# Adding U1 into two banks at mid-block, and giving out mLSTM's key scaling and turn at other steps, in a hybrid mLSTM and DeltaNet layer

## The chip, the cores and the metric

One NeuronCore of a Trainium2 chip runs the whole layer in one launch. Its engines work side by side, each on its own stream of instructions: TensorE (PE in the profile; PEld is its weight load), VectorE (DVE), ScalarE (ACT), GpSimd (POOL) and SyncE (SP, here only a queue that issues DMAs). They wait for each other by semaphores. The metric is the device time of one execution in microseconds (us), as the median of several runs.

## The reference: one layer on 512 tokens of width 2048

A layer normalises x, projects it once, runs two token mixers on the parts of that projection, projects both results back, gates and merges them, adds the residual and normalises. All is fp32, for one batch of 512 tokens and D_MODEL 2048.

```python
IN_SIZES = (ML_QK_WIDTH, ML_QK_WIDTH, ML_WIDTH, ML_WIDTH, ML_WIDTH, ML_HEADS, ML_HEADS,
            3 * DN_WIDTH, DN_WIDTH, DN_HEADS, DN_HEADS,
            D_MODEL, D_MODEL)
...
def _mlstm_chunkwise(q, k, v, i_pre, logf):
...
        num = (inter_w[..., None] * jnp.einsum('bhtd,bhde->bhte', q_c, C)
               + jnp.einsum('bhts,bhse->bhte', intra_w, v_c))
...
        kw = k_c * jnp.exp(we_c - m_new[..., None])[..., None]
        C_new = decay[..., None, None] * C + jnp.einsum('bhsd,bhse->bhde', kw, v_c)
```

The mLSTM has 8 heads with keys of 128 and values of 256; the DeltaNet 16 heads of 128. Most of the work is the two projections: 2048 by some 20,500 columns in, 4096 by 2048 out.

## The kernel before: seven products instead of eight, and a clock of steps

**Precision.** Every fp32 operand of a projection is split into a high and a low part in a format that TensorE multiplies fast; a product of two is then three matmuls (high by high, high by low, low by high). ScalarE casts the high part of a weight tile (L135, `wh`), VectorE subtracts to get the low part (L138, `wl`), from raw tiles that SP loads (`wr`). `uh` and `ul` are the two parts of the normalised input.

**Seven-product blocks.** Nine blocks of two times 512 columns (4 of kind "z", 2 "v", 3 "g": the list SEVEN) are projected by a form of Strassen-Winograd multiplication: the 512 tokens are two halves, the 2048 rows of the weights eight pairs of tiles, and a block of 2 x 2 quarter products is computed with seven products. Each block walks eight quads of group A, with products m6, m1, m5 and m7 each, and then eight quads of group B, with m1, m5 and m7 only, added into the same banks. Each product has two token tiles t of three matmuls of 128x512, so 56 products in all. The operands of group A need sums of the inputs (`suh`, `sul`, `s4h`, `s4l`, made by `u_sums` before the blocks) and sums of weight tiles (`t13`, `ts`, L526, L527), one of which goes to DRAM (`t_d`) and is read again by group B (L533).

All eight PSUM banks of a core are in use by one block: m6 has two (`pso`), and m1, m5 and m7 have two each (`psj` and `psw`). Results are sums of the products. U1[t] and C22[t] are two pairs of tiles in SBUF. At the end of group A, m6 is copied to U1 (L562, ScalarE); then VectorE makes U1 += m1, C22 = U1 + m5 and C22 += m7 (all by `add`, L558). The banks of m1, m5 and m7 go on collecting through group B. At the block's end VectorE adds U1 into m5's banks (m5 = U1 + m5) and m7's to U1 (U1 += m7), and the sinks write out four results per t: m1's bank, m5's bank, C22 and U1, with an activation on ScalarE. The last products of a block come in another order (the last two quads' m1 and m5 before their m7), so that banks of the next block come free early.

**Order.** TensorE's order is the order in which the code calls it, written by hand. The other engines' order comes from a scheduler with priorities: `urgent(n)` raises that of what is inside, loads and splits of the blocks have a high one, and `behind("V")` holds an instruction until the newest split on that engine has been issued. Work beside the products is written as generators: `start(gen, wait)` enters one in a list, and `tick()`, called after each product and each group of projection matmuls, lets each go on to its next `yield n`, n ticks later. So numbers of ticks decide where such work is put against TensorE's.

**mLSTM.** A unit treats two heads j. `ml_start` turns the keys of both heads (by `turn`: a transpose of blocks on VectorE, L774, then four stores to DRAM, L784, and four ticks later one load back, L789) and loads v. `ml_prep` makes decay weights (`em`, L1063) and scores (`psc`, L1068). `ml_rec` scales the turned keys (`kw`, L1087) and runs over four chunks c: `pnum` (L1092) from the scores and the state, and `pcs` (L1098), which needs the scaled keys, for the state of the next chunk. `ml_fin` turns the result out. The first unit (`ml_first`, heads 0 and 1) begins right behind the last seven-product block from keys and queries computed earlier; the other three follow between the DeltaNet units, whose projections (`proj_cm`, L249 to L251, copied from their banks to `yp` at L740) fill TensorE in the meantime.

Of the kernel before, what the change touches and what calls it, by code (L numbers as in the profile page):

```python
# [56 lines left out]
def hybrid_body(  # L57
# [82 lines left out]
    def behind(eng):  # L140

        return tc.issue_after(newest[eng])
# [67 lines left out]
    def start(gen, wait=0):  # L210
        active.append([gen, clock["t"] + wait])
# [167 lines left out]
    def u_sums():  # L379
        for i in range(KH):  # L380
            uf, sf = X[:, 0, :, :], X[:, 1, :, :].rearrange("p a (b n) -> p (a b) n", n=HP)
            V.tensor_tensor(out=uf, in0=uh[:, 2 * i:2 * i + 2, :].bitcast(F32), in1=ul[:, 2 * i:2 * i + 2, :].bitcast(F32),
                            op=ALU.add)
            a11, a21, a12, a22 = uf[:, 0, 0:HP], uf[:, 0, HP:S], uf[:, 1, 0:HP], uf[:, 1, HP:S]
            G.tensor_tensor(out=sf[:, 0], in0=a21, in1=a22, op=ALU.add)
            G.tensor_tensor(out=sf[:, 1], in0=sf[:, 0], in1=a11, op=ALU.subtract)
            G.tensor_tensor(out=sf[:, 2], in0=a11, in1=a21, op=ALU.subtract)
            G.tensor_tensor(out=sf[:, 3], in0=a12, in1=sf[:, 1], op=ALU.subtract)
            yield 3
            for hi, lo, src in ((suh[:, i], sul[:, i], sf[:, 0:3]), (s4h[:, i], s4l[:, i], sf[:, 3])):  # L390
                A.copy(hi, src)
                V.tensor_tensor(out=lo, in0=src, in1=hi.bitcast(F32), op=ALU.subtract)
            yield 2

    acol = cp.tile([P, NC, MLH], F32, tag="acol", name="acol")
    emcol = cp.tile([P, NC, MLH], F32, tag="emcol", name="emcol")
# [159 lines left out]
    def add(x, a, b):  # L556
        with urgent(3):
            V.tensor_tensor(out=x, in0=a, in1=b, op=ALU.add)  # L558

    def copy1(t, p1):  # L560
        with urgent(3):
            A.copy(U1[t], p1)  # L562

    def seven(n0, kind, c1, c2):

        m6, m1, m5, m7 = ([pool.tile([P, NO], F32, tag=t, name="ps") for pool, t in banks_] for banks_ in (OO, JW, JW, JW))
        ends = {"A": (lambda t: copy1(t, m6[t]), lambda t: add(U1[t], U1[t], m1[t]),
                      lambda t: add(C22[t], U1[t], m5[t]), lambda t: add(C22[t], C22[t], m7[t])),
                "B": SINK[kind](c1, c2, m1, m5, m7, n0 + 2 * KH == len(quads))}

        def product(n, m):
            g, i = "AB"[n // KH], n % KH
            ps = ((m6, m1, m5, m7) if g == "A" else (m1, m5, m7))[m]
            hi, lo = partq[n0 + n][m]
            for t in range(2):
                ah, al = LHS[g][m](i, slice(t * P, (t + 1) * P))
                T.matmul(ps[t], ah, hi, start=(g == "A" and i == 0), stop=False, skip_group_check=True)  # L577
                T.matmul(ps[t], ah, lo, start=False, stop=False, skip_group_check=True)  # L578
                T.matmul(ps[t], al, hi, start=False, stop=(i == KH - 1), skip_group_check=True)  # L579
                if i == KH - 1 and ends[g][m] is not None:  # L580
                    ends[g][m](t)
            tick()

        N = 2 * KH
        for n in range(N - 2):
            prep_sums(n0 + n + 1)
            prep_pair(n0 + n + 1)
            load_quad()
            if n == N - 3:

                prep_sums(n0 + n + 3)
            for m in range(4 if n < KH else 3):
                if n == N - 3 and m == 2:
                    prep_sums(n0 + N - 1)
                    prep_pair(n0 + N - 1)
                product(n, m)

        load_quad()
        last = n0 + N == len(quads)
        for n, m in ((N - 2, 0), (N - 2, 1), (N - 1, 0), (N - 1, 1), (N - 2, 2), (N - 1, 2)):  # L600
            if (n, m) == (N - 1, 0):
                prep_pair(n0 + N)
                load_quad()
            if last and (n, m) == (N - 1, 1):
                limit[0] = len(plan)
                prepare(nfront - 1)
            product(n, m)
# [4 lines left out]
    def sink_flat(dst, func, scale):  # L612

        def sink(c1, c2, m1, m5, m7, last):
            def out_(ps, c, col):
                o = spare(last)
                with urgent(3):
                    A.activation(o, ps, func, scale=scale)
                nc.scalar.dma_start(dst(c, col), o)

            def late(x_, c, col):
                with behind("A"):
                    if func != AF.Copy:
                        A.activation(x_, x_, func, scale=scale)
                    nc.scalar.dma_start(dst(c, col), x_)
                yield 1

            def end5(t):
                add(m5[t], U1[t], m5[t])
                out_(m5[t], t, c2)  # L630
                start(late(C22[t], 2 + t, c2), 1)

            def end7(t):
                add(U1[t], U1[t], m7[t])
                start(late(U1[t], 2 + t, c1), 2)

            return (lambda t: out_(m1[t], t, c1)), end5, end7
        return sink

    def sink_z(c1, c2, m1, m5, m7, last):  # L640

        col = c1 - ML_Z
        zs, os_ = {}, {}

        def end1(t):
            zs[t] = spare(False)
            with urgent(3):
                A.copy(zs[t], m1[t])

        def end5(t):  # L650
            add(m5[t], U1[t], m5[t])
            os_[t] = spare(False)
            with urgent(3):
                A.activation(os_[t], m5[t], AF.Tanh, scale=0.5)
            start(late(zs[t], os_[t], t), 5 + 5 * t)

        def late(z, o, c):
            th = spare(True)
            with behind("A"):
                A.activation(th, z, AF.Tanh, scale=0.5)  # L660
                if c > 1:
                    A.activation(o, o, AF.Tanh, scale=0.5)
            with behind("V"):
                V.scalar_tensor_tensor(out=z, in0=th, scalar=1.0, in1=z, op0=ALU.add, op1=ALU.mult)
            yield 2
            with behind("V"):
                V.scalar_tensor_tensor(out=z, in0=o, scalar=1.0, in1=z, op0=ALU.add, op1=ALU.mult)
            yield 2
            with behind("A"):
                nc.scalar.dma_start(g_d[c, :, col:col + NO], z)  # L670

        def end7(t):
            add(U1[t], U1[t], m7[t])
            start(late(U1[t], C22[t], 2 + t), 14 + 5 * t)

        return end1, end5, end7

    SINK = {"g": sink_flat(lambda c, col: tg_d[c, :, col - GATE:col - GATE + NO], AF.Tanh, 0.5),
            "v": sink_flat(lambda c, col: v_d[c, :, col - ML_V:col - ML_V + NO], AF.Copy, 1.0),
# [53 lines left out]
    def bc(col, n):  # L733
        return col.unsqueeze(2).to_broadcast([P, NC, n])
# [316 lines left out]
    def ml_prep(j, hs, kq, u):  # L1051
# [25 lines left out]
        G.tensor_tensor(out=qi, in0=qi, in1=iwb, op=ALU.mult)  # L1077
        u["em"].append((w, we, de, qi))

    def ml_rec(j, hs, kq, u):  # L1080
        h = hs[j]
        v1 = u["v1"][j]
        kT = kq[j][:, 0, :]
        w, we, de, qi = u["em"][j]
        kw = u["kw"][j]
        with behind("V"):
            V.tensor_tensor(out=kw, in0=kw, in1=bc(we, P), op=ALU.mult)  # L1087
        sq = wk.tile([P, NC], F32, tag="sq", name="sq")
        c1 = None
        for c in range(NC):  # L1090
# [18 lines left out]
            jk = wk.tile([P, NB], F32, tag="jk", name="mjk", bufs=1)  # L1109
            A.activation(jk, v1[:, c, 0:NB], AF.Square, accum_out=sq[:, c:c + 1])  # L1110
            if c == NC - 2:
                g = [wk.tile([P, NC, P], F32, tag="g", name="mg", bufs=4) for _ in range(2)]
                for i in range(2):
                    col = h * NB + i * P
                    nc.sync.dma_start(g[i], g_d[:, :, col:col + P].rearrange("c p n -> p c n"))
# [25 lines left out]
    def ml_both(hs, kq, u):  # L1141
        for j in range(2):
            yield from ml_prep(j, hs, kq, u)
        for j in range(2):
            yield from ml_rec(j, hs, kq, u)
            yield from ml_fin(j, hs, u)

    def ml_start(hs, kq, u):
        for j in range(2):
            kw = wk.tile([P, NC, P], F32, tag="ke", name="kw", bufs=4)  # L1150
            turn(kq[j][:, 0, :], kw)
            u["kw"].append(kw)
            v1 = wk.tile([P, NC, NB + 1], F32, tag="aq", name="v1", bufs=4)
            G.memset(v1[:, :, NB:NB + 1], 1.0)
            nc.sync.dma_start(v1[:, :, 0:NB], v_d[:, :, hs[j] * NB:(hs[j] + 1) * NB].rearrange("c p n -> p c n"))
            u["v1"].append(v1)
# [6 lines left out]
    def ml_first(hs, kq, u):  # L1163

        for j in range(2):
            for i in range(2):
                nc.sync.dma_start(kq[j][:, 1 - i, :], qk_d[2 * i + j])
        yield 4
        with behind("V"):
            ml_start(hs, kq, u)  # L1170
        yield 5
        yield from ml_both(hs, kq, u)

    def ml_unit(p):
# [186 lines left out]
```

## Time and profile before

| | us |
|---|---|
| median of 3 runs | 2278.94 (2275.77 to 2279.93) |
| the profiled execution | 2278.73 |
| its span, first to last instruction | 2276.9 |
| TensorE busy in the span | 2218.0 |
| the nine seven-product blocks | 136 to 843 from the span's start |
| first mLSTM unit | from 850 |

In the rows of a group, "x72 | 46.0, 679" means 72 instructions, 46.0 us in all, 679 ns each. Names left and right of the arrow are what is written and read, then come partitions x elements. X stands for a tile of a name with a number (U1, C22). On a timeline, the first two numbers are the start in us from the span's start and the duration, and what stands in brackets is the idle time of the engine ahead of the instruction, and what ended it. A row of the windows view has the length of a stretch, then the busy time of PE, PEld, DVE, ACT and POOL with counts, the clock granted to TensorE as a share of the full one, the DMA engines' share and GB/s. Matmuls are pipelined: their durations overlap, and what one costs is the distance between starts.

### The profile page before, as it was taken

To read this page: it belongs to the slowest core of one execution; us is meant where nothing else is said; L and a number is where in the kernel's file an instruction comes from. 1 tells how busy PE (TensorE), PEld (TensorE's weight loads), DVE (VectorE), ACT (ScalarE), POOL (GpSimd) and SP (SyncE) were. 2 spreads that over 40 slices of the span, in tenths; PEclk is the share of its full clock that TensorE was granted. 3 is DMA by queue.
4 is the path that set the end of the run, shared out by engine and by line. 5 is a ranking of instruction groups with operands and counts; after the bars stand their busy time and mean duration, and the time that the engine had idled before them with its cause. 6 is when DMAs were issued, how large, how long until landed. Compare 5 with 4: busy or idle time off the path is not lost.

```text
span 2276.9 us, 32977 instructions
## 1 busy us (share of the span) xinstructions
PE 2218.0 (97%) x11600; PEld 1858.0 (82%) x11600; DVE 1507.5 (66%) x2725; ACT 893.3 (39%) x1776; POOL 248.3 (11%) x325
## 2 busy tenths in 40 slices
PE   7999999999999999999999999999999999999998
PEld 5888888778778778788888888888888899978886
DVE  5967798777777757776496846867376855334445
ACT  4434444444444443343343434434334334232223
POOL 0500000000000001211021202212022100000111
PEclk9999999999999999999999999999999999999999
DMA  5366666667767757557565746658366556764333
GB/s 157 88 190 188 212 195 213 195 197 232 225 186 221 244 180 201 132 120 197 121 165 121 185 124 155 149 121 204 100 159 144 129 144 201 243 206 149 115 116 131
DMA packets 503464, 384.50 MB, mean 169 GB/s; under 512 B 238337, under 2 KB 402402, under 8 KB 503298
## 3 DMA queue, kind: packets, MB, share of 16 engines
q1 hardware_dynamic: 406018, 333.03, 52.5%
q10 hardware_dynamic: 97280, 49.37, 7.4%
q8 instruction: 91, 1.49, 0.3%
q14 instruction: 75, 0.61, 0.1%
HBM read 309.86 MB, written 72.42 MB: 168 GB/s over the span
## 4 chain that ended last, share of the span: by engine, by line
PE 75%; DMA 9%; DVE 8%; issue 3%; SPq 2%; ACT 1%; POOL 0%; ACTq 0%; DVEq 0%; POOLq 0%
PE pj L249 12%; PE pj L250 11%; PE pj L251 11%; PE ps L578 7%; PE ps L577 6%; PE ps L579 6%; PE py L1295 3%; PE py L1296 3%; PE py L1294 3%; DVE wl L138 3%; DMA wr<-in_w_in_dram 2%; DMA wr<-t_d 2%; PE pjt L264 2%; PE pjt L266 2%; PE pjt L267 2%
## 5 line engine op out<-in xcount | busy, mean ns | idle before, releaser
L138 DVE TENSOR_TENSOR wl<-wr,wh 128x512 fp32r<-128x512 f32 (+1 forms) x624 | 487.2, 786 | 346.0 <-ACT wh L135 336.0
L135 ACT CAST wh<-wr 128x512 fp32r<-128x512 f32 (+1 forms) x624 | 415.6, 669 | 760.3 <-PE pj L250 351.8
L249 PE MATMUL pj<-uh,wh 128*128 128x512 f32 x1280 | 531.1, 415 | 3.2 <-ACT yp L740 3.2
L251 PE MATMUL pj<-uh,wl 128*128 128x512 f32 x1280 | 501.8, 392 | 0.0
L250 PE MATMUL pj<-ul,wh 128*128 128x512 f32 x1280 | 501.3, 392 | 0.0
L251 PEld LDWEIGHTS pj<-uh,wl 128*128 128x128 f32 x1280 | 241.1, 188 | 53.0
L249 PEld LDWEIGHTS pj<-uh,wh 128*128 128x128 f32 x1280 | 242.0, 189 | 49.0 <-ACT yp L740 4.0
L250 PEld LDWEIGHTS pj<-ul,wh 128*128 128x128 f32 x1280 | 242.1, 189 | 43.1
L578 PE MATMUL ps<-wl,uh 128*128 128x512 f32 x432 | 170.6, 395 | 7.1 <-DVE wl L138 7.1
L577 PE MATMUL ps<-wh,uh 128*128 128x512 f32 x432 | 169.6, 393 | 2.5 <-DVE X L558 2.3
L579 PE MATMUL ps<-wh,ul 128*128 128x512 f32 x432 | 168.3, 390 | 0.0
L578 PE MATMUL ps<-wl,suh 128*128 128x512 f32 x432 | 168.1, 389 | 0.0
L577 PE MATMUL ps<-wh,suh 128*128 128x512 f32 x432 | 168.1, 389 | 0.0
L579 PE MATMUL ps<-wh,sul 128*128 128x512 f32 x432 | 168.1, 389 | 0.0
L264 PE MATMUL pjt<-wh,uh 128*128 128x256 f32 x512 | 149.1, 291 | 4.5 <-ACT tgs L696 2.7
L266 PE MATMUL pjt<-wl,uh 128*128 128x256 f32 x512 | 146.7, 287 | 0.4 <-DVE wl L138 0.4
L267 PE MATMUL pjt<-wh,ul 128*128 128x256 f32 x512 | 146.4, 286 | 0.0
L135 ACT CAST wh<-ts 128x512 fp32r<-128x512 f32 x144 | 88.9, 617 | 144.3 <-DVE ts L533 106.5
L135 ACT CAST wh<-t 128x1024 fp32r<-128x1024 f32 x72 | 75.8, 1053 | 160.7 <-PE ps L579 91.2
L138 DVE TENSOR_TENSOR wl<-ts,wh 128x512 fp32r<-128x512 f32 x144 | 98.2, 685 | 23.5 <-ACT wh L135 23.5
L138 DVE TENSOR_TENSOR wl<-t,wh 128x1024 fp32r<-128x1024 f32 x72 | 88.0, 1223 | 33.6 <-ACT wh L135 33.2
L578 PEld LDWEIGHTS ps<-wl,uh 128*128 128x128 f32 x432 | 81.1, 188 | 31.0 <-DVE wl L138 15.6
(286 smaller groups left out, 3691.8 us busy)
## 6 DMA issues: line engine op xcount, KB each, us to landing
wr<-in_w_in_dram SPq DMA_DIRECT2D x712, 256.0 KB, 3.5
wr<-in_w_out_dram SPq DMA_DIRECT2D x128, 256.0 KB, 3.1
t_d<-ts ACTq DMA_DIRECT2D x72, 256.0 KB, 3.7
wr<-t_d SPq DMA_DIRECT2D x72, 256.0 KB, 4.0
tgl<-tg_d SPq DMA_DIRECT2D x24, 256.0 KB, 3.6
xt<-in_x_dram SPq DMA_DIRECT2D x8, 512.0 KB, 7.4
v<-v_d SPq DMA_DIRECT2D x8, 512.0 KB, 5.9
gb<-rows_d SPq DMA_DIRECT2D x16, 256.0 KB, 4.1
```

The costliest lines, as they stand in the source:

```text
L135: newest["A"] = A.copy(hi, src).ins
L138: newest["V"] = V.tensor_tensor(out=lo, in0=src, in1=hi.bitcast(F32), op=ALU.subtract).ins
L249: T.matmul(ps[j], hi[:, k, wsl], uh[:, kt, :], start=(kt == 0), stop=False)
L250: T.matmul(ps[j], hi[:, k, wsl], ul[:, kt, :], start=False, stop=False)
L251: T.matmul(ps[j], lo[:, k, wsl], uh[:, kt, :], start=False, stop=(kt == KT - 1))
L264: T.matmul(o, uh[:, kt, tsl], hi[:, k, :], start=(kt == 0 and c % 2 == 0), stop=False, skip_group_check=True)
L266: T.matmul(o, uh[:, kt, tsl], lo[:, k, :], start=False, stop=False, skip_group_check=True)
L267: T.matmul(o, ul[:, kt, tsl], hi[:, k, :], start=False, stop=(kt == KT - 1), skip_group_check=True)
L577: T.matmul(ps[t], ah, hi, start=(g == "A" and i == 0), stop=False, skip_group_check=True)
L578: T.matmul(ps[t], ah, lo, start=False, stop=False, skip_group_check=True)
L579: T.matmul(ps[t], al, hi, start=False, stop=(i == KH - 1), skip_group_check=True)
L1294: T.matmul(ps[c], hh[base][:, kt, tsl], hi[:, 0, :], start=(kt == 0), stop=False)
```

## The change

Three edits.

1. In `u_sums` the two yields 3 and 2 become 4 and 1.
2. In the seven-product blocks U1 is added into the banks of m5 and m7 between group A and group B. `add5` makes C22 = U1 + m5 and ScalarE copies C22 into m5's bank; `add7` makes C22 += m7 and m7 = U1 + m7 in its bank. The sinks are then four functions: m5's and m7's banks hold results when group B ends, m7's is copied or activated into U1 by ScalarE (`end21`), and C22 is given out from mid-block on (`end22`, at once for kinds "v" and "g" with 3 + t ticks to wait; for "z" it leaves with U1 as before).
3. In mLSTM the key scaling becomes a function, `scale_kw`: for head 0 it is called ahead of both recurrences, with a yield of 1 behind it, and for head 1 at chunk NC - 2 of head 0's recurrence. In `ml_first`, `ml_start` treats one head at a time, with a yield of 5 behind each, where it treated both and yielded 5 once.

```diff
@@ u_sums
-            yield 3
+            yield 4
             for hi, lo, src in ((suh[:, i], sul[:, i], sf[:, 0:3]), (s4h[:, i], s4l[:, i], sf[:, 3])):
                 A.copy(hi, src)
                 V.tensor_tensor(out=lo, in0=src, in1=hi.bitcast(F32), op=ALU.subtract)
-            yield 2
+            yield 1
@@ seven
+        end11, end12, end21, end22 = SINK[kind](c1, c2, m1, m5, m7, n0 + 2 * KH == len(quads))
+
+        def add5(t):
+            add(C22[t], U1[t], m5[t])
+            with urgent(3):
+                A.copy(m5[t], C22[t])
+
+        def add7(t):
+            add(C22[t], C22[t], m7[t])
+            add(m7[t], U1[t], m7[t])
+            end22(t)
+
         ends = {"A": (lambda t: copy1(t, m6[t]), lambda t: add(U1[t], U1[t], m1[t]),
-                      lambda t: add(C22[t], U1[t], m5[t]), lambda t: add(C22[t], C22[t], m7[t])),
-                "B": SINK[kind](c1, c2, m1, m5, m7, n0 + 2 * KH == len(quads))}
+                      add5, add7),
+                "B": (end11, end12, end21)}
...
-                if i == KH - 1 and ends[g][m] is not None:
+                if i == KH - 1:
                     ends[g][m](t)
@@ sink_flat (kinds "v" and "g")
-            def end5(t):
-                add(m5[t], U1[t], m5[t])
-                out_(m5[t], t, c2)
-                start(late(C22[t], 2 + t, c2), 1)
-
-            def end7(t):
-                add(U1[t], U1[t], m7[t])
-                start(late(U1[t], 2 + t, c1), 2)
-
-            return (lambda t: out_(m1[t], t, c1)), end5, end7
+            def end21(t):
+                with urgent(3):
+                    A.activation(U1[t], m7[t], func, scale=scale)
+                nc.scalar.dma_start(dst(2 + t, c1), U1[t])
+
+            return (lambda t: out_(m1[t], t, c1), lambda t: out_(m5[t], t, c2), end21,
+                    lambda t: start(late(C22[t], 2 + t, c2), 3 + t))
@@ sink_z
-        def end5(t):
-            add(m5[t], U1[t], m5[t])
+        def end12(t):
             os_[t] = spare(False)
...
-        def end7(t):
-            add(U1[t], U1[t], m7[t])
+        def end21(t):
+            with urgent(3):
+                A.copy(U1[t], m7[t])
             start(late(U1[t], C22[t], 2 + t), 14 + 5 * t)
 
-        return end1, end5, end7
+        return end11, end12, end21, lambda t: None
@@ mLSTM
+    def scale_kw(j, u):
+        kw, we = u["kw"][j], u["em"][j][1]
+        with behind("V"):
+            V.tensor_tensor(out=kw, in0=kw, in1=bc(we, P), op=ALU.mult)
+
     def ml_rec(j, hs, kq, u):
...
         kw = u["kw"][j]
-        with behind("V"):
-            V.tensor_tensor(out=kw, in0=kw, in1=bc(we, P), op=ALU.mult)
...
             if c == NC - 2:
+                if j == 0:
+                    scale_kw(1, u)
...
     def ml_both(hs, kq, u):
         for j in range(2):
             yield from ml_prep(j, hs, kq, u)
+        scale_kw(0, u)
+        yield 1
...
-    def ml_start(hs, kq, u):
-        for j in range(2):
+    def ml_start(hs, kq, u, js=(0, 1)):
+        for j in js:
...
         yield 4
-        with behind("V"):
-            ml_start(hs, kq, u)
-        yield 5
+        for j in range(2):
+            with behind("V"):
+                ml_start(hs, kq, u, (j,))
+            yield 5
         yield from ml_both(hs, kq, u)
```

More of the change, by code (lines that the diff above doesn't have):

```diff
@@ L643, in sink_z, with end11 @@
         zs, os_ = {}, {}
-        def end1(t):
+        def end11(t):
             zs[t] = spare(False)
```

## The prediction, made before the changed kernel had run

> **What bounds the kernel now.** I read the page first, then PE's waits, then the nine seven-product blocks stretch by stretch, then timelines at the places that the change touches.
>
> ```profile
> span 2276.9 us, 32977 instructions
> PE 2218.0 (97%) x11600; PEld 1858.0 (82%) x11600; DVE 1507.5 (66%) x2725; ACT 893.3 (39%) x1776; POOL 248.3 (11%) x325
> ```
>
> TensorE is the bound: what counts is only how long it stands still, and at what clock it runs. All that it waited for by name in the places that the change touches:
>
> ```profile
> PE ps L578 <- DVE wl L138: 7.1, 12, 1.4
> PE pcs L1098 <- DVE kw L1087: 4.4, 3, 3.4
> PE pj L249 <- ACT yp L740: 3.2, 2, 2.3
> PE ps L577 <- DVE X L558: 2.3, 8, 0.6
> ```
>
> The columns are total us, times and the longest wait. The mid-block adds (the last row) cost 2.3 us in the whole run, so there is little to win there. The windows view, cut at the nine blocks (136 to 843 us), ends in this line:
>
> ```profile
> sum 707.00, PE 697.27 PEld 565.66 DVE 546.63 ACT 312.50 POOL 0.00; mean PE 77.47 PEld 62.85 DVE 60.74 ACT 34.72 POOL 0.00
> ```
>
> PE stands still for only 707.00 - 697.27 = 9.7 us in all blocks together. A new stall there can be made good by at most that much.
>
> **Part 1: the adds.** Before, a block has six DVE adds between its halves and four at its end. After, it has eight between the halves and none at the end, and ScalarE copies C22 back into the two m5 banks. The rows that carry the prices, from the view of groups:
>
> ```profile
> L558 DVE TENSOR_TENSOR X<-X,ps 128x512 f32<-128x512 f32 x72 | 46.0, 679 | 1.3 <-PE ps L579 1.3
> L558 DVE TENSOR_TENSOR ps<-X,ps 128x512 f32<-128x512 f32 x18 | 12.3, 686 | 2.6 <-PE ps L579 2.6
> L562 ACT COPY X<-ps 128x512 f32<-128x512 f32 x18 | 9.6, 582 | 0.0
> ```
>
> The 18 adds that vanish (one less for each of two halves in nine blocks) are 18 x 0.68 = 12.2 us of DVE work, at block ends where no row shows PE waiting for them: worth nothing. A ScalarE copy *into* a bank is not in this trace. From a bank it took 582 ns; the adds show that writing a bank instead of SBUF costs 686 against 679 ns. I take 0.58 us and bound it by 0.58 and 0.69.
>
> What matters is the middle. In block 1, PE starts the second half's m1 at 257.70 us and runs to the end of the adds like this (DVE, then ScalarE, then PE):
>
> ```profile
> 255.97 0.69 DVE L533 TENSOR_TENSOR ts<-wr 128x512 f32<-128x512 f32 x1
> 256.58 1.88 DVE L558 TENSOR_TENSOR X<-X,ps 128x512 f32<-128x512 f32 x3
> 258.37 0.68 DVE L138 TENSOR_TENSOR wl<-ts,wh 128x512 fp32r<-128x512 f32 x1
> 258.97 1.28 DVE L558 TENSOR_TENSOR X<-X,ps 128x512 f32<-128x512 f32 x2
> 260.26 0.69 DVE L533 TENSOR_TENSOR ts<-wr 128x512 f32<-128x512 f32 x1
> 260.87 0.68 DVE L558 TENSOR_TENSOR X<-X,ps 128x512 f32<-128x512 f32 x1
> 261.47 1.22 DVE L138 TENSOR_TENSOR wl<-wr,wh 128x1024 fp32r<-128x1024 f32 x1
> 262.60 0.68 DVE L138 TENSOR_TENSOR wl<-ts,wh 128x512 fp32r<-128x512 f32 x1
> ```
> ```profile
> 257.90 1.06 ACT L135 CAST wh<-wr 128x1024 fp32r<-128x1024 f32 x1 [0.53 <-PE ps L579]
> ```
> ```profile
> 257.70 0.39 PE L577 MATMUL ps<-wh,uh 128*128 128x512 f32 x1
> 259.74 0.46 PE L577 MATMUL ps<-wh,s4h 128*128 128x512 f32 x1
> 261.60 0.49 PE L577 MATMUL ps<-wh,uh 128*128 128x512 f32 x1 [0.23 <-DVE X L558]
> ```
>
> Starts in a row lie 0.60 us apart for 128x512 and 1.13 us for 128x1024 (261.47 to 262.60). PE's half-products (three matmuls) lie 0.68 us apart: m1, m1, m5, then the second m5 at 259.74, m7, the second m7. The last of these started at 261.60 instead of 261.2, behind the sixth add (260.87 + 0.68).
>
> In the changed program's instruction order DVE runs here: both U1 adds, add5 of half 0, wl, add5 of half 1, both adds of add7 for half 0, ts, the 1024-wide wl, both adds for half 1. ScalarE runs: m5 copy of half 0, the 1024-wide cast, m5 copy of half 1. Replayed from the same 256.58:
>
> - add5 of half 0 ends at 258.46, its copy at 259.05, in time. The cast, now behind that copy, runs 259.0 to 260.0; the second copy, behind the cast, ends near 260.55. The second m5 half-product wanted 259.74: a stall of 0.8 us.
> - Two adds for m7 of half 0 end at 260.85, in time. Then ts (260.8), wl (261.4), and the last two adds from 262.5: the second ends at 263.75. PE, already 0.8 late, wants the second m7 at 261.95: a stall of 1.8 us.
>
> So that half-product starts near 263.8 instead of 261.60; a further 0.2 is won back, as small waits behind it vanish: 2.0 us. DVE's order in blocks 0 and 5 to 8 has both add5 together, and the same replay there gives 2.09, 2.09, 2.08, 2.05 and 2.09; blocks 1 to 4 give 1.97, 2.07, 2.09 and 2.10 (estimates, all from their own rows as above). Sum over nine: +18.6 us.
>
> **What is won back later in the block.** The split chain that feeds PE hangs on loads, not on PE, at one place some 28 us after the middle, for example in block 5:
>
> ```profile
> 588.45 0.69 DVE L533 TENSOR_TENSOR ts<-wr 128x512 f32<-128x512 f32 x1 [2.49 <-DMA wr<-t_d]
> 596.84 1.23 DVE L526 TENSOR_TENSOR t<-wr 128x1024 f32<-128x1024 f32 x1 [3.65 <-DMA wr<-in_w_in_dram]
> ```
>
> The loads' order is unmoved, so a PE that comes 2 us later finds the data there. That swallows most of the 7.1 us of `ps <- wl` above: I take -6.5, bounded by 0 (the loads slip with PE, as their buffers come free later) and by -9.7, all of PE's idle time in the blocks.
>
> **The clock.** Windows of 3.41 us, laid end to end:
>
> ```profile
> 79.95:83.37 3.42, 1.56 (x14) 1.36 (x13) 3.28 (x8) 2.40 (x5) 1.52 (x3) 1.00 0.44 119
> 83.37:86.78 3.41, 3.41 (x19) 3.41 (x18) 3.41 (x6) 0.95 (x2) 1.78 (x2) 0.50 0.64 193
> 598.78:602.19 3.41, 2.04 (x9) 1.35 (x9) 3.41 (x6) 3.27 (x6) 0.00 (x0) 1.00 0.52 170
> 602.19:605.60 3.41, 3.41 (x17) 2.82 (x16) 3.41 (x5) 0.61 (x2) 0.00 (x0) 1.00 0.90 287
> 865.02:868.43 3.41, 1.13 (x6) 0.76 (x5) 1.49 (x3) 3.21 (x8) 0.32 (x2) 1.00 0.96 212
> 868.43:871.85 3.42, 3.42 (x14) 3.03 (x13) 3.42 (x6) 0.92 (x3) 1.13 (x2) 0.50 1.02 277
> 929.87:933.28 3.41, 2.42 (x6) 1.99 (x7) 3.41 (x9) 1.81 (x5) 0.00 (x0) 0.50 0.94 168
> 933.28:936.70 3.42, 3.42 (x10) 2.65 (x9) 2.68 (x6) 0.11 (x2) 0.00 (x0) 0.50 0.69 139
> ```
>
> The second column is PE busy, the third from the end the granted clock. After a window with 1.56 us busy, or 1.13, the next one ran at 0.50; after 2.04 it did not. Half the clock for 3.41 us costs 1.7 us of work. The changed middle stands still for 0.8, works 1.36 (two half-products), stands still for 1.8: a window that holds it best has 3.41 - 2.05 = 1.36 busy, plus some 0.3 for two tails (a lone matmul counts 0.39, not 0.23); a window that a stall is cut by has more than 2. So it lies between the two rows, and where the windows fall decides: I take 4 to 5 of 9 blocks, +7.5 us, bounded by 0 and 9 x 1.7 = 15.3.
>
> The Trainium skill's "TensorE: Matmul & The Clock Gate" (section "Part 1: The HAM clock gate (the "warmup" mystery)") drops the clock only after at least one idle window of about 3.4 us. By that rule stalls of 1.8 us drop nothing, and the sum would be 7.5 us lower. The rows above disagree with it: the window at 79.95 was not idle, with 1.56 us busy.
>
> **Part 2: mLSTM.** Two stalls with a lowered clock behind each stand where the change moves work:
>
> ```profile
> 864.87 0.39 PE L251 MATMUL pj<-uh,wl 128*128 128x512 f32 x1
> 867.54 0.50 PE L249 MATMUL pj<-uh,wh 128*128 128x512 f32 x1 [2.28 <-ACT yp L740]
> 927.05 0.39 PE L251 MATMUL pj<-uh,wl 128*128 128x512 f32 x1
> 930.86 1.20 PE L1098 MATMUL pcs<-v,kw 128*128 128x257 f32 x2 [3.42 <-DVE kw L1087]
> ```
> ```profile
> 852.90 9.02 SPq L784 DMA_DIRECT2D td<-kw  x8
> 862.03 0.95 SPq L171 DMA_DIRECT2D wr<-in_w_in_dram  x2
> ```
> ```profile
> 865.22 0.62 ACT L135 CAST wh<-wr 128x512 fp32r<-128x512 f32 x1 [6.33 <-DMA wr<-in_w_in_dram]
> 866.92 0.56 ACT L740 COPY yp<-pj 128x512 f32<-128x512 f32 x1
> ```
>
> - First stall: the weight load stands on SP's queue behind eight turn stores (9.02 us); its cast and the copy that frees the bank are late by it. Splitting the turn by head puts four stores ahead of that load and four later, so it goes out some 4.5 us sooner, more than the 2.4 us lost (867.54 - 864.87 - 0.23). With 1.7 for the halved window: -4.1.
> - Second stall: DVE reaches the scaling of kw for head 1 only after the work of head 0. Given out three chunks' steps earlier, it is long done. 930.86 - 927.05 - 0.23 = 3.6, and at half clock (929.87 to 936.70, of which PE stood still until 930.86) 2.9: -6.5.
> - The other two waits of that row: 4.4 - 3.4 = -1.0.
>
> Together -11.6, of which I take -11, since the recurrences begin one step later and the scaling of head 0 has only about 2 us in hand (an estimate from the order). The bounds are 0 and -11.6. The four stores that come later hold SP's queue for 4.5 us (half of 9.02) in a stretch where no row shows PE waiting for a load.
>
> **Part 3: u_sums' yields (3, 2 to 4, 1).** The sum of yields is unmoved, and the instruction order of every engine is the same up to the first block's middle: 0.
>
> **Sum.** 2278.73 (the profiled execution, 0.2 below the median of 2278.94) + 18.6 - 6.5 + 7.5 - 11 = 2287.3: **2287 us**, 0.4% slower.
>
> **Rivals.**
>
> - *The stalls come, the clock holds.* 2278.73 + 18.6 - 6.5 - 11 = 2279.8: no change that can be told. For it: the window at 598.78 kept its clock. Against: two stalls fall in one window here. The rule of the Trainium skill's page named above would end here. Chance 0.20.
> - *Faster: the supply runs ahead, so the adds start sooner.* In block 1 the first U1 add begins at 256.58, behind a ts, though its bank was full near 255.1 (two products of 1.36 us ahead of 257.70). If loads do not slip with PE, the ts is done sooner against PE in every block but the first, and all eight adds move up by as much as 1.5 us: the first stall vanishes, the second falls to 0.3 or so, 0.75 a block against before, 6.7 in all, below what is won back later; no window halves. 2278.73 + 6.7 - 6.5 - 11 = about 2268. It decides from a lead of 1 us on. For it: DVE's waits on loads above. Against: the raw buffers come free by casts that wait for PE (`257.90 ... <-PE ps L579`), so the chain follows PE. Chance 0.20.
> - *Worse.* Nothing is won back later, and most blocks lose a window (7 x 1.7 = 12): 2278.73 + 18.6 + 12 - 11 = 2298. For it: buffers freed later by a late PE. Chance 0.15.
> - *The change does not do what it says*: the adds could stay where they were if the scheduler moved them back. The order above shows eight at mid-block; excluded.
>
> **How the numbers follow.** The forecast (some windows halved) has 0.45. This kernel's runs lie within 0.2%, 4.6 us, so that bounds "no change": 2274 to 2283.5. Faster 0.20 (second rival), same 0.20 (the first), slower 0.60 (forecast and third). The range goes from the second rival's 2268 to 2300, a little above the third; beyond it lie only 15.3 us of clock with nothing won back. The forecast's own range is 2282 to 2294.
>
> **What would show it.** Right: in each block PE waiting about 0.8 us for the ScalarE copy and about 1.8 us for a DVE add into ps, some 2.6 x 9 = 23 us of such waits; `ps <- wl` below 2 us; granted clock 0.50 behind four or five middles; the waits for kw L1087 and for yp at 867 gone, with their halved windows. Wrong: middles without waits (second rival), a clock of 1.00 behind all of them (first), or new waits past 850 us where pcs and pj stood, which would take the 11 us back.

## The result, and the profile after

| | before | after |
|---|---|---|
| median of 13 runs each, us | 2275.63 | 2285.96 |
| profiled execution: span, us | 2276.9 | 2285.6 |
| ratio of the times, 95% interval | | 1.0047 (1.0036 to 1.0058) |

The change made the kernel slower by 0.47% (0.36 to 0.58), some 10.7 us. The page, and PE's waits inside the blocks (130 to 870 us; total us, times, longest):

```profile
span 2285.6 us, 32979 instructions
PE 2216.0 (97%) x11600; PEld 1856.4 (81%) x11600; DVE 1508.0 (66%) x2707; ACT 909.4 (40%) x1806; POOL 256.9 (11%) x325
```
```profile
PE ps L589 <- DVE ps L558: 15.1, 9, 2.4
PE ps L589 <- ACT ps L572: 4.2, 11, 0.5
PE ps L590 <- DVE wl L138: 3.1, 6, 1.1
PE ps L589 <- DVE X L558: 2.2, 3, 1.3
```

Two waits are new. PE waits for a DVE add into a bank once in each of the nine blocks (15.1 us), and for the ScalarE copy into m5's banks (4.2 us); the forecast had named 1.8 us and 0.8 us a block, 16.2 and 7.2 in all. The old wait for the split of weights (`ps <- wl`) fell from 7.1 to 3.1 us. The windows view, again cut at the nine blocks (now 136 to 856 us), ends so:

```profile
sum 720.00, PE 694.90 PEld 563.84 DVE 541.86 ACT 327.20 POOL 0.00; mean PE 77.21 PEld 62.65 DVE 60.21 ACT 36.36 POOL 0.00
```

PE stands still for 720.00 - 694.90 = 25.1 us in the blocks; it was 9.7. So the blocks cost 15.4 us more, and everything behind them gives 2285.6 - 2276.9 - 15.4 = -6.7 us. First the middle of block 1, on DVE, ScalarE and PE:

```profile
257.02 1.88 DVE L558 TENSOR_TENSOR X<-X,ps 128x512 f32<-128x512 f32 x3
258.81 0.68 DVE L138 TENSOR_TENSOR wl<-ts,wh 128x512 fp32r<-128x512 f32 x1
259.41 1.27 DVE L558 TENSOR_TENSOR X<-X,ps 128x512 f32<-128x512 f32 x2
260.61 0.69 DVE L558 TENSOR_TENSOR ps<-X,ps 128x512 f32<-128x512 f32 x1
262.01 0.69 DVE L533 TENSOR_TENSOR ts<-wr 128x512 f32<-128x512 f32 x1 [0.71 <-DMA wr<-t_d]
262.62 1.22 DVE L138 TENSOR_TENSOR wl<-wr,wh 128x1024 fp32r<-128x1024 f32 x1
263.75 0.68 DVE L558 TENSOR_TENSOR X<-X,ps 128x512 f32<-128x512 f32 x1
264.35 0.69 DVE L558 TENSOR_TENSOR ps<-X,ps 128x512 f32<-128x512 f32 x1
```
```profile
258.93 0.59 ACT L572 COPY ps<-X 128x512 f32<-128x512 f32 x1 [1.11 <-DVE X L558]
259.45 1.04 ACT L135 CAST wh<-wr 128x1024 fp32r<-128x1024 f32 x1
260.40 0.58 ACT L572 COPY ps<-X 128x512 f32<-128x512 f32 x1
```
```profile
258.72 0.39 PE L589 MATMUL ps<-wh,uh 128*128 128x512 f32 x1
261.04 0.50 PE L589 MATMUL ps<-wh,s4h 128*128 128x512 f32 x1
265.09 0.50 PE L589 MATMUL ps<-wh,uh 128*128 128x512 f32 x1 [2.40 <-DVE ps L558]
```

The second m5 half-product starts 2.32 us behind 258.72 (2.04 would be without a wait): the copy behind the cast is late, as forecast, though by 0.28 us and not by 0.8 in this block. The second m7 half-product starts at 265.09, 6.37 us behind it, where it was 3.90 before. Ahead of the last pair of adds DVE runs a ts and a 1024-wide wl, and here the ts waits 0.71 us for its load while both adds stand behind it, ready: DVE runs in order.

Behind the blocks the two stalls of the first mLSTM unit are gone. The same matmul (a projection's) on both sides, before and after:

```profile
948.43 0.59 PE L249 MATMUL pj<-uh,wh 128*128 128x512 f32 x1
```
```profile
953.51 0.39 PE L249 MATMUL pj<-uh,wh 128*128 128x512 f32 x1
```

Of the 15.4 us, 10.3 have been won back there (953.51 - 948.43 = 5.1 left). Then a new stall stands at 960.57, with a halved clock behind it (the last line below, a window of 3.41 us):

```profile
960.57 0.39 PE L251 MATMUL pj<-uh,wl 128*128 128x512 f32 x1
963.19 0.50 PE L249 MATMUL pj<-uh,wh 128*128 128x512 f32 x1 [2.23 <-ACT thz L769]
963.99:967.41 3.42, 3.42 (x10) 2.68 (x9) 0.00 (x0) 1.95 (x4) 0.69 (x5) 0.50 0.63 173
```
```profile
959.06 0.71 DVE L783 STREAM_TRANSPOSE to<-v 128x512 f32<-128x512 f32 x1 [2.80 <-DMA hm_d<-to]
```
```profile
959.81 1.63 ACTq L793 DMA_DIRECT2D hm_d<-to  x3
961.53 0.62 ACT L135 CAST wh<-wr 128x512 fp32r<-128x512 f32 x1 [4.86 <-DMA td<-to]
962.53 0.60 ACT L769 ACTIVATE thz<-pj 128x512 f32<-128x512 f32 x1
```

Read from PE back: PE waits for a bank that ScalarE has not emptied; ScalarE stands behind the stores of a turned result (`hm_d`), which wait for DVE's transpose; DVE waits 2.80 us for one of the two buffers `to`, whose stores have not landed. Both engines run in order here, so everything behind waits too.

### The profile page after: what moved, and what is told of

The parts are those of the page before. It is cut to its first block, busy times and chain, and to the rows that moved or that the text cites. A ratio compares the mean times of both kernels' runs of the same rounds, so it can differ in the third digit from the quotient of the medians.

```text
span 2285.6 us, 32979 instructions
## 1 busy us (share of the span) xinstructions
PE 2216.0 (97%) x11600; PEld 1856.4 (81%) x11600; DVE 1508.0 (66%) x2707; ACT 909.4 (40%) x1806; POOL 256.9 (11%) x325
## 4 chain that ended last, share of the span: by engine, by line
PE 69%; DMA 12%; DVE 11%; issue 3%; SPq 2%; ACT 2%; ACTq 0%; POOL 0%; DVEq 0%; POOLq 0%
PE pj L249 10%; PE pj L250 10%; PE pj L251 10%; PE ps L590 7%; PE ps L589 7%; PE ps L591 7%; DVE wl L138 4%; PE py L1312 3%; PE py L1313 3%; PE py L1311 3%; DMA wr<-t_d 2%; DMA wr<-in_w_in_dram 2%; DMA hr<-h_d 1%; DMA hr<-hm_d 1%; ACT wh L135 1%
## 5 line engine op out<-in xcount | busy, mean ns | idle before, releaser
L589 PE MATMUL ps<-wh,uh 128*128 128x512 f32 x432 | 169.8, 393 | 17.4 <-DVE ps L558 15.1
L589 PEld LDWEIGHTS ps<-wh,uh 128*128 128x128 f32 x432 | 81.1, 188 | 39.8 <-DVE ps L558 19.0
```

## The experiments

Each kernel was timed in five rounds beside the kernel before; ratios are to it, with the 95% interval.

**The parts alone.** `s_only` has only the seven-product edit, `ml_only` both mLSTM edits, `kw_only` only the moved scaling, `split_only` only the split turn, `us_only` only the two yields of `u_sums`. Their edits are those hunks of the diff above.

> The seven-product edit alone (mLSTM and u_sums as before). Theory: it costs what the two traces differ by at the end of the blocks, 15.5 us, ratio about 1.0068; PE waits of 15 us for DVE adds into ps and 4 us for the ScalarE copies, and the stall at pcs and the one at yp as before. Rival (the adds are nearly free, and it is the moved mLSTM work that made the kernel slower): within 3 us of before, ratio under 1.0015.

Measured: 1.0068 (1.0053 to 1.0083), 2288.72 us. That is the theory's number: the whole loss is the seven-product edit's. Its trace has 15.3 us of waits for the adds into ps, 4.7 for the copies. The two mLSTM stalls did not stay as before, though that code is unchanged: the wait at yp is absent from this trace, and the one for the scaled keys is 5.2 us long instead of 3.4.

> Both mLSTM edits alone (blocks and u_sums as before). Theory: -11 us for the waits at yp and at kw with their halved windows, +4 for a new stall that the changed kernel's trace shows at 960.6 (a bank copy on ScalarE behind the stores of head 0's turned-out result), so -6 to -8 us, ratio about 0.997. Rival (the new stall belongs to the later arrival from the blocks, not to the mLSTM edit): the full -11, ratio 0.995.

Measured: 0.9978 (0.9965 to 0.9991), -5 us. At the kernel's matmul that stood at 948.43 the lead is 14 us in its trace; then about 5 go back at a wait for thz of 2.7 us with a halved window. So the new stall belongs to the mLSTM edits themselves, not to the late arrival from the blocks.

> Only the key scaling given out elsewhere; both heads' turn together as before. Theory: the wait for the scaled keys of head 1 is gone with its halved window, -6.5, and the two later pcs waits, -1; the wait at yp with its halved window stays; the recurrences come one step later only, so the new stall at the turned-out result does not come: -7.5, ratio 0.9967. Rival: without the split turn the same wait only moves to another engine's row: within 2 us.

Measured: 0.9996 (0.9986 to 1.0007): the rival. The wait for the scaled keys is gone, and others stand in its place:

```profile
PE pnum L1097 <- DVE c L1107: 2.1, 1, 2.1
PE pj L249 <- ACT yp L740: 1.7, 1, 1.7
PE pnum L1097 <- DVE c L1105: 1.7, 1, 1.7
```

These are the waits from 840 to 1000 us of this kernel. Up to 931 us it leads by 9.3 us; the state's copy (`c`) comes late from DVE twice, and the second time the clock is halved behind it.

> Only the turn of the first unit split by head; key scaling as before. Theory: the wait at yp with its halved window is gone, -4.1; the wait for the scaled keys of head 1 stays in some size; the recurrences come five steps later, so the new stall of the turned-out result (+4) comes: between -4 and +1. Rival (the stall comes from the scaling's place, not from the five steps): -4.1 and no stall where the result is turned out.

Measured: 0.9986 (0.9978 to 0.9995), -3 us, in the range. The wait at yp is gone (0.5 us left in the run), a wait of 2.59 us for the scaled keys stays:

```profile
934.57 1.23 PE L1098 MATMUL pcs<-v,kw 128*128 128x257 f32 x2 [2.59 <-DVE kw L1087]
937.31 0.71 DVE L774 STREAM_TRANSPOSE to<-v 128x512 f32<-128x512 f32 x1 [0.76 <-DMA td<-to]
```

The new stall, which the theory counted in, did not come: DVE waits 0.76 us for a buffer `to` when it turns the result, and PE does not wait for `thz` at all. In this the rival was right. The wait for `thz` (2.2 us in the changed kernel, 2.7 in `ml_only`) stands in the traces of both mLSTM edits together, and in that of neither alone.

> Only the two yields of u_sums. Theory: nothing, ratio 1.000 within 0.001. Rival (it sets the first block off differently): beyond 0.001 either way.

Measured: 1.0005 (0.9993 to 1.0016): no change that can be told. The three parts multiplied, 1.0068 x 0.9978 x 1.0005 = 1.0051, make up the whole, 1.0047.

**What in the middle costs.** Four kernels vary the seven-product edit, with mLSTM and `u_sums` as before; the edits of `hold` and `raw_copy` are shown against the changed kernel, those of `m5_only` and `m7_only` against the kernel before. `hold` keeps two DVE instructions of the weights' split behind the last mid-block add:

```diff
-            add(m7[t], U1[t], m7[t])
+            newest["7"] = add(m7[t], U1[t], m7[t])
...
+                with (tc.issue_after(newest["7"]) if i == 3 else ExitStack()):
                     V.tensor_tensor(out=ts[:, 0, :], in0=r[:, 0, :], in1=r[:, 2, :], op=ALU.subtract)
...
-            with tc.high_priority(offset=2 * PRIO):
+            with tc.high_priority(offset=2 * PRIO), (tc.issue_after(newest["7"]) if quads[q][4:] == ("B", 1) else ExitStack()):
                 w2 = split(pair, True)
```

> The seven-product edit alone, with one change: the ts of the fourth quad of group B and the 1024-wide wl of its second quad may not be issued on DVE before the last mid-block add. Theory (the second stall is DVE's order, two instructions of 0.6 and 1.14 us among the adds): the last add ends near 262.05 instead of 263.75 in block 1, PE loses 0.5 to 0.9 us a block against the kernel before instead of 2, and the whole costs +3 to +6 us, ratio 1.0013 to 1.0026. Rival (what costs is the ScalarE copy, or the number of adds): no better than the edit alone, ratio 1.0068.

Measured: 0.9997 (0.9986 to 1.0009), 2276.13 us: better than expected. With eight adds at mid-block and both ScalarE copies, the edit has no cost that can be told. DVE in block 1:

```profile
257.35 1.87 DVE L559 TENSOR_TENSOR X<-X,ps 128x512 f32<-128x512 f32 x3
259.15 0.68 DVE L138 TENSOR_TENSOR wl<-ts,wh 128x512 fp32r<-128x512 f32 x1
259.75 1.27 DVE L559 TENSOR_TENSOR X<-X,ps 128x512 f32<-128x512 f32 x2
260.94 0.68 DVE L559 TENSOR_TENSOR ps<-X,ps 128x512 f32<-128x512 f32 x1
261.54 0.67 DVE L559 TENSOR_TENSOR X<-X,ps 128x512 f32<-128x512 f32 x1
262.14 0.68 DVE L559 TENSOR_TENSOR ps<-X,ps 128x512 f32<-128x512 f32 x1
262.74 1.21 DVE L138 TENSOR_TENSOR wl<-wr,wh 128x1024 fp32r<-128x1024 f32 x1
263.88 0.68 DVE L534 TENSOR_TENSOR ts<-wr 128x512 f32<-128x512 f32 x1
```

The same instructions, only in another order: the last add ends at 262.82, and PE's second m7 half-product starts at 262.88 in its trace, 3.82 us behind 259.06, the start of the second half, against 6.37 in the changed kernel and 3.90 in the kernel before. Its blocks' waits hold none for an add into ps any more. Not every stall is gone: by the starts of the same products, the nine middles take 4.3 us more than before in this trace (21.0 more in `s_only`), 2.4 of them in the last block, where PE waits 1.5 us for an add to U1 and the clock is halved behind it; 2.9 us are won back elsewhere in the blocks.

> The seven-product edit alone, but without an add that waits for ScalarE: ScalarE copies the raw m5 bank to C22 as soon as group A is through with it, DVE adds U1 in place into m5 and then m7, and C22 += m7's new bank comes last. Still eight DVE adds and two ScalarE copies a block, and in the issue order the ts and the 1024-wide wl still stand ahead of the last add. Theory (DVE's order): the last add ends near 263.7 as before this variation, +15 us, ratio 1.006 to 1.007, though no wait for a ScalarE copy is left. Rival (the chain add, copy, add through ScalarE costs it): 1.002 or less.

```diff
         def add5(t):
-            add(C22[t], U1[t], m5[t])
             with urgent(3):
-                A.copy(m5[t], C22[t])
+                A.copy(C22[t], m5[t])
+            add(m5[t], U1[t], m5[t])
 
         def add7(t):
-            add(C22[t], C22[t], m7[t])
             add(m7[t], U1[t], m7[t])
+            add(C22[t], C22[t], m7[t])
             end22(t)
```

Measured: 1.0102 (1.0086 to 1.0119), +23 us: no chain through ScalarE is left, and it is slower still. The rival (that this chain is what costs) falls; the theory has the sign, but is 8 us short. In this order both additions to C22, which read m7's banks, come last, behind ts and wl, so both m7 halves stay blocked: in block 1 PE's half-products start 2.93 us apart there instead of 0.68, so it stands still for 2.25 us in one piece; in four of the nine blocks the clock is then halved, as in block 2:

```profile
345.09:348.50 3.41, 1.30 (x6) 1.01 (x6) 3.41 (x5) 1.56 (x2) 0.00 (x0) 1.00 0.21 41
348.50:351.92 3.42, 3.42 (x10) 2.66 (x9) 1.75 (x3) 0.00 (x0) 0.00 (x0) 0.50 1.00 292
```

> Only m5's half of the seven-product edit: add5 with its ScalarE copy at mid-block, U1 += m7 at the block's end as before; mLSTM and u_sums as before. Six adds at mid-block, but the issue order now has ts and the 1024-wide wl ahead of the last of them (in the kernel before only ts). Theory (DVE's order): the last add ends near 263.1, PE's second m7 half-product loses 1.5 us a block, +10 us net, ratio 1.0045. Rival (the number of adds decides): six adds as before, so under +4 us, ratio under 1.0015.

```diff
         def end5(t):
-            add(m5[t], U1[t], m5[t])
             out_(m5[t], t, c2)
```

(with `add5` at mid-block and `add7` left out.) Measured: 1.0106 (1.0091 to 1.0121), +24 us, more than the whole edit. It is no matter of the number of adds, which is six as before; but the middle explains only part. Worked out from the starts of the same products, the middles cost 8.6 us (1 us a block, where 1.5 was expected) and the rest of the blocks 14.0, where the changed kernel wins 4.1 back. Its waits in the blocks:

```profile
PE ps L583 <- DVE wl L138: 15.9, 14, 3.0
PE ps L582 <- DVE X L558: 6.6, 12, 1.3
PE ps L582 <- ACT ps L570: 4.9, 12, 0.5
```

The late place in the block, where DVE waits for loads, became worse; in block 3 for example a DVE t waits 5.28 us for its load, and 2.82 at the same place in `s_only`. Why the loads come later there was not settled.

> Only m7's half: U1 is added into m7's banks at mid-block, m5's at the block's end as before, no ScalarE copy at mid-block; mLSTM and u_sums as before. Eight adds at mid-block, with only ts (none in five blocks) among the last of them. Theory (DVE's order): the last add ends near 262.6, 1 us a block lost, +5 to +7 us net, ratio 1.0022 to 1.003. Rival (the number of adds decides): eight as in the whole edit, so +15 us, ratio 1.0068.

```diff
-                      lambda t: add(C22[t], U1[t], m5[t]), lambda t: add(C22[t], C22[t], m7[t])),
+                      lambda t: add(C22[t], U1[t], m5[t]), add7),
...
         def end7(t):
-            add(U1[t], U1[t], m7[t])
-            start(late(U1[t], 2 + t, c1), 2)
+            with urgent(3):
+                A.activation(U1[t], m7[t], func, scale=scale)
+            nc.scalar.dma_start(dst(2 + t, c1), U1[t])
```

Measured: 1.0041 (1.0026 to 1.0057), +9 us, between theory and rival but nearer the theory; its trace has 6.8 us in the middles. Eight adds, and some 40% less loss than the whole edit (0.41% against 0.68%). That fits the theory, by which only ts stands among them; but this kernel also leaves out the ScalarE copies, so it does not separate the two by itself.

**Towards a better kernel.** `ml_fin4` is `ml_only` with `yield 4` for `yield 1` in `ml_fin`; `hold_ml` is `hold` with the mLSTM edits; `hold_ml_fin4` has both.

> Both mLSTM edits, blocks and u_sums as before, and a yield of 4 instead of 1 behind each turn of a result in ml_fin. Theory (the edits give back 4 to 6 us because the second turned half of head 0's result waits for a buffer whose stores have not gone out, and DVE and ScalarE stand behind it): three steps more and the buffer is free, so the 2.7 us wait at the copy of thz and its halved window go, -8 to -10 us, ratio 0.996. Rival (DVE is short of time in this stretch, and any spacing only moves the wait): as with the two edits alone, 0.9978, with another wait of 2 us or more between 910 and 960.

Measured: 0.9992 (0.9978 to 1.0005): no better than without (0.9978; the intervals overlap), and its trace has the longer wait, so the guess about the spacing fell.

```profile
944.48 0.71 DVE L774 STREAM_TRANSPOSE to<-v 128x512 f32<-128x512 f32 x1 [4.60 <-DMA td<-to]
```
```profile
948.57 0.80 PE L249 MATMUL pj<-uh,wh 128*128 128x512 f32 x1 [5.01 <-ACT thz L760]
```

The second half of the result now waits for a buffer that a DeltaNet turn took (`td`, not `hm_d`), and longer. Two buffers `to` serve the mLSTM's result and the DeltaNet's values (vt) alike. A third one was not tried.

> The seven-product edit with the ts and wl held behind the last mid-block add, and both mLSTM edits; u_sums as before. Theory (the parts add up): 0.9997 x 0.9978 = 0.9975, -5.7 us. Rival (the parts meet, since the mLSTM unit starts where the blocks leave it): 1.000 or more.

Measured: 0.9983 (0.9974 to 0.9992), 2271.77 us: faster than both kernels, and the same as `ml_only` (0.9978) within the intervals. The parts add up.

> The kernel above with the yield of 4 in ml_fin: what the fix of each part is worth together. Theory: 0.9997 x 0.996 = 0.9957, -10 us. Rival: no better than without the yields, 0.9975.

Measured: 0.9994 (0.9983 to 1.0005): the rival, as after `ml_fin4`.

## Why the prediction came out right, and where its sum did not

2287 us was forecast, 8.3 us above the profiled execution; the traces differ by 8.7 and the runs by 10.7. That the sum was right is luck: the clock, 7.5 us too high, was cancelled by the mLSTM term, 7.8 us too low, and the two terms of the blocks, together 3.5 us too low, by 4.1 us in a stretch that no edit touches.

| term | predicted, us | in the traces, us |
|---|---|---|
| stalls in the nine middles | +18.6 | +19.7 |
| won back later in the block | -6.5 | -4.1 |
| clock halved behind the middles | +7.5 | 0 |
| mLSTM | -11 | -10.3 up to 950 us, of which 7 are given back by 2000 us: -3.2 |
| output projection (`py`, from 2000 us on) | not in it | -4.1 |
| u_sums | 0 | 0 |

The last column is worked out from the starts of the same matmuls in both traces. It adds up to 8.3; the other 0.4 us of the 8.7 lie behind the last of these matmuls. The row of the output projection is the traced execution's and not the change's: PE's waits for the split of its weights are 2.5 + 1.7 us in the trace before and 0.6 + 0.4 in the changed kernel's, but also 0.5 + 0.4 in `s_only` and 0.3 + 0.3 in `us_only`, whose mLSTM is the old one. In the runs the mLSTM edits are worth about 5 us (`ml_only`, and 1.0047 against the 1.0068 of `s_only`).

- **The stalls in the middles** were right in size and cause. `hold` shows the cause: with the two DVE instructions behind the adds the loss is gone, though the adds, the copies and the loads are the same. The first stall (the copy behind the 1024-wide cast) is there too, but `hold` keeps it (3.5 us of waits); in its block 1 it costs nothing, because PE then waits for the last add, which ends at 262.82, all the same. The replay did not have DVE waiting for a load among the adds, as in block 1.
- **Won back later** was mis-sized by 2.4 us, inside the bounds given: `ps <- wl` fell by 4.0, not by most of 7.1.
- **The clock** is the step that failed: "it lies between the two rows, and where the windows fall decides: I take 4 to 5 of 9 blocks". None of nine was halved. A row of the middles that came nearest, with the window behind it:

```profile
182.34:185.75 3.41, 1.66 (x6) 1.05 (x6) 3.41 (x6) 1.75 (x3) 0.00 (x0) 1.00 0.06 7
185.75:189.16 3.41, 3.33 (x15) 2.76 (x16) 1.75 (x3) 0.00 (x0) 0.00 (x0) 1.00 0.93 244
```

  1.66 us of PE busy kept the clock, and 1.56 had lost it: the limit lies close to what these stalls leave. The forecast had the best-placed window right (1.36 us and some 0.3 for tails), but how many blocks reach the limit was a guess, and it was far too high. Counted by the distance between starts, as in the last section, PE stands still for 2.05 us in the first of these windows, and no window of 3.41 us laid anywhere over eight of the nine middles holds more than 2.13 us. So where the windows fall decides much less than was thought. Only block 1, where ts waits for its load, leaves room for 2.68 us, and in this trace its stall is split between two windows. In `s_only`, with the same blocks, one window holds 2.41 us of standing still there, and the next one is halved:

```profile
263.54:266.95 3.41, 1.13 (x5) 0.96 (x6) 3.41 (x5) 1.56 (x2) 0.00 (x0) 1.00 0.37 105
266.95:270.37 3.42, 3.42 (x10) 2.65 (x9) 1.30 (x3) 0.62 (x1) 0.00 (x0) 0.50 0.83 268
```

  In these two traces 1 of 18 middles was halved, where half of them were expected: the term was 0 and 1.7 us, not 7.5. The first rival had this right, though not its time of 2280, which had the full -11 in it. The Trainium skill's "TensorE: Matmul & The Clock Gate" (section "Part 1: The HAM clock gate (the "warmup" mystery)") would also have had no halving here; but it asks for a whole idle window, and `raw_copy` (PE busy for 1.30 of 3.41 us) shows that it takes less.
- **mLSTM**: 10.3 us were won by 950 us, about the 11 that were forecast. But the prices "-4.1" and "-6.5" were read from one execution. Six more traces have the old mLSTM code (`s_only`, `us_only`, `hold`, `raw_copy`, `m5_only`, `m7_only`): in them the wait at yp is between 0 and 2.0 us and has no halved window behind it, and the wait for the scaled keys is 4.6 to 5.7 us; their way from the end of the blocks to the matmul at 948.43 is 0.7 to 2.9 us shorter than in the trace before. The step that failed is "in a stretch where no row shows PE waiting for a load": the later stores and the later recurrence were looked at as load on SP's queue, not as users of the two buffers `to`. With both edits the recurrence of the first unit begins six steps later, its result is turned in the midst of the DeltaNet's turns, and DVE and ScalarE stand behind a buffer. `split_only` begins five steps later and has no such stall on PE, so the later start alone does not bring it; why it takes both edits was not settled. In time the two edits add within the noise (0.9996 x 0.9986 = 0.9982, together 0.9978), but each brings less than forecast: where its stall is removed or made shorter, the next wait comes from another row.
- **The faster rival** (supply ahead, adds sooner) did not come: in block 1 the first U1 add starts 1.70 us ahead of the second half's first matmul, where it started 1.12 ahead. That is 0.6 us sooner, and the 1 us from which that rival decides is not reached; in blocks 2 to 4 the lead stays at 0.73 to 0.77. In block 1 DVE's wait for the ts load also holds up the last two adds.

## What to carry to other kernels

Where several instructions must end before an accumulation can go on, look at what the scheduler has put among them on an in-order engine: here two split instructions, 1.7 us, not the two extra adds, decided 15 us over nine blocks. Work moved off a stall takes along its buffers; list who else uses them at the new place before counting the stall as won. A stall that is read from one execution may be smaller or absent in the next, so its price is worth looking up in a second trace. And a sum that comes out right is no proof of its terms: check each one in the trace.

## What the runs showed of the hardware

In these traces the clock of TensorE is decided by how much of a fixed window of 3.41 us it stands still in all, not by one long pause. In the traces of all fourteen kernels, with each matmul of 512 columns counted as 0.227 us and the others by their columns, and the first 25 us and the end left out: of the windows at full clock in which PE stood still for 2.3 us or more, all 24 were followed by one at half clock; between 2.0 and 2.3 us, 18 of 28; between 1.2 and 2.0 us, none of 179. Among those followed by half clock is one with no pause of 1 us: its two longest are 0.98 and 0.94 us, of 2.16 in all (`raw_copy`, 184.67):

```profile
184.67:188.08 3.41, 1.82 (x7) 0.86 (x7) 3.41 (x6) 1.57 (x2) 0.00 (x0) 1.00 0.00 0
188.08:191.49 3.41, 3.41 (x9) 2.63 (x10) 1.56 (x2) 0.00 (x0) 0.00 (x0) 0.50 0.88 235
```

PE busy is no sharp measure for it: 1.82 us lost the clock here, and 1.66 kept it above, since a matmul alone counts 0.39 us busy while one in a row takes 0.227. It is the distance between starts that has to be counted.
